# Binary cross entropy with 8-bit targets: VectorE negates both halves of a chunk, and only then clips the next chunk

## The chip, the cores and the metric

The kernel runs on one core of a Trainium2 chip. The metric is the device time of one execution in microseconds (us), shown as the median of several runs. A profile is taken of one more execution.

## The reference

For two float32 arrays of 8192 x 8192, `pred` in (0, 1) and `target` of zeros and ones, the kernel computes the binary cross entropy of every element:

```python
def reference(pred, target):
    eps = 1e-7
    pred = np.clip(pred, eps, 1 - eps)
    return -(target * np.log(pred) + (1 - target) * np.log(1 - pred))
```

As `target` is 0 or 1, one of the two products is always zero. The result is -log(p) where the target is 1 and -log(1 - p) where it is 0. The kernel uses this: |target - 1 + p| is p for a target of 1, and 1 - p for a target of 0, so one logarithm per element is enough.

## The kernel before

**Tiling.** Both inputs and the output are taken as one flat run of 128 x 524288 elements and cut into 35 chunks, k = 0 to 34. The first and the last have 8704 elements per partition (`SIDE`), the 33 between them 15360 (`WIDE`). Each chunk is worked on in two halves (`PARTS = 2`), of 7680 elements per partition in a wide chunk and of 4352 in the two short ones.

**Buffers.** `ring_p` holds three chunks of float32 side by side; chunk k lies in slot k mod 3, is changed in place through all its steps, and is stored from there. `ring_t` is one single chunk of targets in uint8: the transfer that loads the targets turns float32 into 8-bit integers on its way, so it reads 7680 KB and writes 1920 KB for a wide chunk.

**Steps of one chunk.** `clip` (line 85, VectorE) limits p to the allowed interval. `merge` (line 91, VectorE) adds target - 1 to it; then ScalarE takes the absolute value (line 94) and the logarithm (line 95). `negate` (line 99, VectorE) multiplies by -1. `store` (line 70) writes the chunk out.

**Who issues transfers.** Nearly all transfers are issued by GpSimd (POOL), one after another in the order in which the program names them: `load_t` (line 67), `store` (line 70), `load_p` (line 63) and the main part of `store_last` (line 74). They all go into queue q0. Only the first load of `pred` is issued by ScalarE, and the last 1024 columns of the last store by SyncE in three pieces (line 77).

**The order by hand.** The program is written in a manual schedule: each engine executes its instructions in the order of the text, and only waits for what it needs. Before the loop, chunk 0 is clipped. The loop over k = 0 to 34 then does, in this order:

1. both merges of chunk k, with the two ScalarE operations behind each;
2. `load_t(k + 1)` on POOL, which must wait until both merges have read the single target buffer;
3. on VectorE, for each half i: `clip(k + 1, i)`, then `negate(k, i)` (lines 118 to 121);
4. on POOL, `store(k)`, which waits for both negations, and then `load_p(k + 2)`, which waits for the store of chunk k - 1, the last user of its slot.

So the first clip in point 3 waits for the load of `pred` of chunk k + 1, and a negation waits for the logarithm of its half. As VectorE works in order, a negation also waits for every clip that stands in front of it.

**The end.** From chunk 32 on the order differs. The store of chunk 32 is not issued in its own step but in the next, between the loads of the two halves of the last chunk's targets (lines 114 to 117). The stores of chunks 33 and 34 come behind the loop (lines 126 and 127).

Of the kernel before, what the change touches and what calls it, by code (L numbers as in the profile page):

```python
# [1 line left out]

# [4 lines left out]

EPS = 1e-7

WIDE = 15360  # L10
SIDE = 8704
SLOTS = 3
PARTS = 2
REST = 1024
ROWS = (108, 12, 8)


@with_exitstack
def kernel(
    ctx: ExitStack,  # L20
    tc: tile.TileContext,
    pred: bass.AP,
    target: bass.AP,
    out: bass.AP,
):
    nc = tc.nc
    fp32 = mybir.dt.float32
    uint8 = mybir.dt.uint8
    Alu = mybir.AluOpType
    Act = mybir.ActivationFunctionType  # L30
    P = nc.NUM_PARTITIONS

    R, C = pred.shape
    total = R * C // P
    n = (total - 2 * SIDE) // WIDE + 2
    widths = [SIDE] + [WIDE] * (n - 2) + [SIDE]
    assert sum(widths) == total
    last = n - 1

    pool = ctx.enter_context(tc.tile_pool(name="rings", bufs=1))  # L40
    ring_p = pool.tile([P, SLOTS * WIDE], fp32, name="ring_p", tag="ring_p")
    ring_t = pool.tile([P, WIDE], uint8, name="ring_t", tag="ring_t")
    warm = pool.tile([1, 8], fp32, name="warm", tag="warm")

    def chunk(ap, k):
        flat = ap.rearrange("r c -> (r c)")
        start = sum(widths[:k]) * P
        return flat[start : start + widths[k] * P].rearrange("(p w) -> p w", p=P)

    def p_of(k, a=0, b=None):  # L50
        c = k % SLOTS * WIDE
        return ring_p[:, c + a : c + (widths[k] if b is None else b)]

    def t_of(k, a=0, b=None):
        return ring_t[:, a : widths[k] if b is None else b]

    def part(k, i):
        w = widths[k]
        return i * w // PARTS, (i + 1) * w // PARTS

    def load_p(k):
        queue = nc.scalar if k == 0 else nc.gpsimd
        queue.dma_start(out=p_of(k), in_=chunk(pred, k))  # L63

    def load_t(k, *cols):
        cols = cols or (0, widths[k])
        nc.gpsimd.dma_start(out=t_of(k, *cols), in_=chunk(target, k)[:, cols[0] : cols[1]])  # L67

    def store(k):
        nc.gpsimd.dma_start(out=chunk(out, k), in_=p_of(k))  # L70

    def store_last():
        w = SIDE - REST
        nc.gpsimd.dma_start(out=chunk(out, last)[:, :w], in_=p_of(last, 0, w))  # L74
        r = 0
        for rows in ROWS:
            nc.sync.dma_start(
                out=chunk(out, last)[r : r + rows, w:], in_=p_of(last, w)[r : r + rows, :]
            )
            r += rows  # L80
        assert r == P

    def clip(k, i):
        p = p_of(k, *part(k, i))
        nc.vector.tensor_scalar(  # L85
            out=p, in0=p, scalar1=EPS, scalar2=1 - EPS, op0=Alu.max, op1=Alu.min
        )

    def merge(k, i):
        p, t = p_of(k, *part(k, i)), t_of(k, *part(k, i))  # L90
        nc.vector.scalar_tensor_tensor(  # L91
            out=p, in0=t, scalar=1.0, in1=p, op0=Alu.subtract, op1=Alu.add
        )
        nc.scalar.activation(out=p, in_=p, func=Act.Abs)  # L94
        nc.scalar.activation(out=p, in_=p, func=Act.Ln)  # L95

    def negate(k, i):
        p = p_of(k, *part(k, i))
        nc.vector.tensor_scalar(out=p, in0=p, scalar1=-1.0, scalar2=None, op0=Alu.mult)  # L99

    with tc.manual_schedule():
        load_p(0)
        load_t(0)
        load_p(1)
        nc.vector.memset(warm, 1.0)  # L105
        nc.scalar.activation(out=warm, in_=warm, func=Act.Ln)  # L106
        for i in range(PARTS):
            clip(0, i)
        for k in range(n):
            for i in range(PARTS):  # L110
                merge(k, i)
            if k < last - 1:
                load_t(k + 1)
            elif k == last - 1:
                load_t(last, 0, SIDE // PARTS)
                store(last - 2)
                load_t(last, SIDE // PARTS, SIDE)
            for i in range(PARTS):
                if k < last:
                    clip(k + 1, i)  # L120
                negate(k, i)
            if k < last - 2:
                store(k)
            if k < last - 1:
                load_p(k + 2)
        store(last - 1)
        store_last()


# [1 line left out]
_INS = ['pred', 'target']  # L131
_OUTS = [((8192, 8192), 'float32')]


# [23 lines left out]
```

## Time and profile before

| | |
|---|---|
| time, median of 3 runs | 1917.45 us (1916.74 to 1917.89) |
| the profiled execution's own time | 1917.1 us |
| its span, first to last instruction | 1915.1 us |
| VectorE (DVE) busy | 1113.2 us (58%) |
| ScalarE (ACT) busy | 899.8 us (47%) |
| GpSimd (POOL) busy | 57.6 us (3%) |
| bytes read from and written to HBM | 536.87 MB and 268.44 MB |

In the groups of instructions, a row names the line, the engine, the operation, what it writes and reads, and its count; then the total busy time and the mean of one instruction in ns. A row of the timeline gives the start and the duration in us, and in brackets how long the engine stood idle before it and what ended the wait. Where equal instructions follow each other, the timeline merges them into one row and gives their number behind an x. A row of a transfer's issue in the timeline is the time that POOL took to issue it, and not the time of the transfer. The latter stands in the list of transfers, as the median time from issue to landing, with the size in KB on the SBUF side. That list can be taken for a short window as well, and then speaks of the one transfer that was issued in it. In the list of waits, a row names who waited for whom, the total in us, how many times, and the longest.

### The profile page before, as it was taken

To read this page: it belongs to the slowest core of one execution; us is meant where nothing else is said; L and a number is where in the kernel's file an instruction comes from. 1 tells how busy PE (TensorE), PEld (TensorE's weight loads), DVE (VectorE), ACT (ScalarE), POOL (GpSimd) and SP (SyncE) were. 2 spreads that over 40 slices of the span, in tenths; PEclk is the share of its full clock that TensorE was granted. 3 is DMA by queue.
4 is the path that set the end of the run, shared out by engine and by line. 5 is a ranking of instruction groups with operands and counts; after the bars stand their busy time and mean duration, and the time that the engine had idled before them with its cause. 6 is when DMAs were issued, how large, how long until landed. Compare 5 with 4: busy or idle time off the path is not lost.

```text
span 1915.1 us, 651 instructions
## 1 busy us (share of the span) xinstructions
DVE 1113.2 (58%) x211; ACT 899.8 (47%) x142; POOL 57.6 (3%) x109
## 2 busy tenths in 40 slices
DVE  4656655555666555566655556665555666555583
ACT  3554334555433455543345554334555433455543
POOL 0000000000000000000000000000000000000000
DMA  9999999999999999999999999999999999999997
GB/s 296 303 350 299 296 308 300 311 354 349 308 287 308 308 303 354 351 306 303 305 295 308 349 354 304 307 308 287 308 354 349 323 287 308 308 287 354 352 281 290
DMA packets 15428, 604.02 MB, mean 315 GB/s; under 512 B 1728, under 2 KB 1728, under 8 KB 2112
## 3 DMA queue, kind: packets, MB, share of 16 engines
q0 software_dynamic: 15120, 599.01, 98.5%
q10 hardware_dynamic: 144, 4.46, 0.6%
q1 hardware_dynamic: 160, 0.52, 0.1%
q14 instruction: 4, 0.03, 0.0%
HBM read 536.87 MB, written 268.44 MB: 421 GB/s over the span
## 4 chain that ended last, share of the span: by engine, by line
DMA 67%; issue 30%; DVE 1%; POOL 0%; POOLq 0%; DVEq 0%; PEldq 0%
DMA ring_t<-in_target_dram 67%; DVE ring_p L91 1%; POOL ring_t L67 0%; POOL out_dram L70 0%; POOLq L153 0%; POOLq L67 0%; POOLq L70 0%; DVEq L91 0%; PEldq L153 0%; POOLq L74 0%
## 5 line engine op out<-in xcount | busy, mean ns | idle before, releaser
L94 ACT ACTIVATE ring_p<-ring_p 128x7680 f32<-128x7680 f32 (+1 forms) x70 | 450.5, 6436 | 991.1 <-DVE ring_p L91 991.1
L85 DVE TENSOR_SCALAR ring_p<-ring_p 128x7680 f32<-128x7680 f32 (+1 forms) x70 | 283.9, 4057 | 701.9 <-DMA ring_p<-in_pred_dram 701.9
L91 DVE SCALAR_TENSOR_TENSOR ring_p<-ring_t,ring_p 128x7680 f32<-128x7680 uint8 (+1 forms) x70 | 554.1, 7956 | 63.1 <-DMA ring_t<-in_target_dram 63.1
L95 ACT ACTIVATE ring_p<-ring_p 128x7680 f32<-128x7680 f32 (+1 forms) x70 | 451.1, 6444 | 2.2
L99 DVE TENSOR_SCALAR ring_p<-ring_p 128x7680 f32<-128x7680 f32 (+1 forms) x70 | 283.8, 4054 | 17.8 <-ACT ring_p L95 17.8
L70 POOL DMA_DIRECT2D out_dram<-ring_p x34 | 18.3, 538 | 1183.5 <-DVE ring_p L99 1183.5
L67 POOL DMA_DIRECT2D ring_t<-in_target_dram x36 | 20.8, 579 | 631.9 <-DVE ring_p L91 631.1
L63 POOL DMA_DIRECT2D ring_p<-in_pred_dram x34 | 18.0, 530 | 2.6 <-DMA out_dram<-ring_p 2.6
L106 ACT ACT_TABLE_LOAD x1 | 1.3, 1283 | 1.1 <-PEq L142 1.1
L74 POOL DMA_DIRECT2D out_dram<-ring_p x1 | 0.5, 538 | 21.8 <-DVE ring_p L99 21.8
L105 DVE MEMSET warm<- 1x8 f32 x1 | 0.1, 65 | 0.8 <-PEq L142 0.8
L106 ACT ACTIVATE warm<-warm 1x8 f32<-1x8 f32 x1 | 0.2, 208 | 0.0
L142 POOL MEMSET const-float32-0.0<- 128x1 f32 x1 | 0.1, 99 | 0.2 <-issue 0.2
L142 POOL MEMSET const-bfloat16-1.0<- 128x1 bf16 x1 | 0.1, 102 | 0.0
L142 POOL MEMSET const-float32-1.0<- 128x1 f32 x1 | 0.1, 99 | 0.0
L142 POOL MEMSET const-uint8-127<- 128x1 uint8 x1 | 0.1, 99 | 0.0
## 6 DMA issues: line engine op xcount, KB each, us to landing
ring_p<-in_pred_dram POOLq DMA_DIRECT2D x33, 7680.0 KB, 38.5
out_dram<-ring_p POOLq DMA_DIRECT2D x33, 7680.0 KB, 20.9
ring_t<-in_target_dram POOLq DMA_DIRECT2D x33, 1920.0 KB, 39.1
ring_p<-in_pred_dram ACTq DMA_DIRECT2D x1, 4352.0 KB, 20.8
out_dram<-ring_p POOLq DMA_DIRECT2D x1, 4352.0 KB, 16.2
ring_p<-in_pred_dram POOLq DMA_DIRECT2D x1, 4352.0 KB, 46.3
out_dram<-ring_p POOLq DMA_DIRECT2D x1, 3840.0 KB, 12.9
ring_t<-in_target_dram POOLq DMA_DIRECT2D x1, 1088.0 KB, 22.9
```

The source lines that it names most:

```text
L63: queue.dma_start(out=p_of(k), in_=chunk(pred, k))
L67: nc.gpsimd.dma_start(out=t_of(k, *cols), in_=chunk(target, k)[:, cols[0] : cols[1]])
L70: nc.gpsimd.dma_start(out=chunk(out, k), in_=p_of(k))
L74: nc.gpsimd.dma_start(out=chunk(out, last)[:, :w], in_=p_of(last, 0, w))
L85: nc.vector.tensor_scalar(out=p, in0=p, scalar1=EPS, scalar2=1 - EPS, op0=Alu.max, op1=Alu.min)
L91: nc.vector.scalar_tensor_tensor(out=p, in0=t, scalar=1.0, in1=p, op0=Alu.subtract, op1=Alu.add)
L94: nc.scalar.activation(out=p, in_=p, func=Act.Abs)
L95: nc.scalar.activation(out=p, in_=p, func=Act.Ln)
L99: nc.vector.tensor_scalar(out=p, in0=p, scalar1=-1.0, scalar2=None, op0=Alu.mult)
L105: nc.vector.memset(warm, 1.0)
L106: nc.scalar.activation(out=warm, in_=warm, func=Act.Ln)
L142: nc = _bacc.Bacc("TRN2", target_bir_lowering=False, num_devices=1)
```

## The change

On VectorE, the two negations of chunk k now come first, in a loop of their own, and the two clips of chunk k + 1 behind them. Before, clips and negations took turns, with a clip first.

```diff
             for i in range(PARTS):
-                if k < last:
+                negate(k, i)
+            if k < last:
+                for i in range(PARTS):
                     clip(k + 1, i)
-                negate(k, i)
             if k < last - 2:
                 store(k)
             if k < last - 1:
```

The instructions are the same, in number and in shape. The order on POOL, ScalarE and SyncE is the same as before. What each instruction waits for is the same too: a negation for the logarithm of its half, the first clip for the load of its chunk, the store for both negations.

## The prediction

> **What bounds the kernel now.** I read the page first (busy shares, queues, transfers), then the waits, then the timeline of one step in the middle. The page and the waits:
>
> ```profile
> span 1915.1 us, 651 instructions
> DVE 1113.2 (58%) x211; ACT 899.8 (47%) x142; POOL 57.6 (3%) x109
> ...
> q0 software_dynamic: 15120, 599.01, 98.5%
> ...
> ring_p<-in_pred_dram POOLq DMA_DIRECT2D x33, 7680.0 KB, 38.5
> out_dram<-ring_p POOLq DMA_DIRECT2D x33, 7680.0 KB, 20.9
> ring_t<-in_target_dram POOLq DMA_DIRECT2D x33, 1920.0 KB, 39.1
> ...
> ring_p<-in_pred_dram POOLq DMA_DIRECT2D x1, 4352.0 KB, 46.3
> ```
> ```profile
> POOL out_dram L70 <- DVE ring_p L99: 1183.5, 33, 37.6
> POOL ring_p L63 <- DMA out_dram<-ring_p: 2.6, 1, 2.6
> ```
>
> No compute engine is near full. Queue q0, which POOL fills, has packets under way for 98.5% of 16 engines' span: the kernel is a stream of three transfers a step (store k, load of pred k+2, load of target k+1), and time can be won only where one of them takes longer than its bytes need. The long wait of stores on the negations (1183.5 us) is therefore not a price by itself. Loads of pred hardly ever wait for their slot (2.6 us, once). One step, from one landing of the targets to the next:
>
> ```profile
> 944.15 16.23 DVE L91 SCALAR_TENSOR_TENSOR ring_p<-ring_t,ring_p 128x7680 f32<-128x7680 uint8 x2 [1.77 <-DMA ring_t<-in_target_dram]
> ...
> 960.67 0.53 POOL L67 DMA_DIRECT2D ring_t<-in_target_dram  x1 [16.94 <-DVE ring_p L91]
> ...
> 972.10 6.60 ACT L95 ACTIVATE ring_p<-ring_p 128x7680 f32<-128x7680 f32 x1
> 981.71 4.16 DVE L85 TENSOR_SCALAR ring_p<-ring_p 128x7680 f32<-128x7680 f32 x1 [21.34 <-DMA ring_p<-in_pred_dram]
> ...
> 993.92 4.15 DVE L99 TENSOR_SCALAR ring_p<-ring_p 128x7680 f32<-128x7680 f32 x1
> 998.37 0.54 POOL L70 DMA_DIRECT2D out_dram<-ring_p  x1 [37.17 <-DVE ring_p L99]
> 998.90 0.53 POOL L63 DMA_DIRECT2D ring_p<-in_pred_dram  x1
> 999.85 16.23 DVE L91 SCALAR_TENSOR_TENSOR ring_p<-ring_t,ring_p 128x7680 f32<-128x7680 uint8 x2 [1.77 <-DMA ring_t<-in_target_dram]
> ```
>
> A merge or a clip that waits for a transfer starts with its landing, so its start dates the landing to about 0.1 us. The period is 999.85 - 944.15 = 55.70 us. The load of targets takes 999.85 - 981.71 = 18.14 us behind the load of pred. Store and load of pred together take 981.71 - 944.15 = 37.56. The store issued at 998.37 lands 20.9 us later, at 1019.27; the load of pred issued at 998.90 lands at 1037.4, so it takes 18.1 by itself, and the store the other 19.5. Store and loads move the same 7680 KB on the float side, so **the store takes about 1.4 us more than its bytes**. Its place says why: it is issued 1.5 us before the targets land, after which the queue has nothing else. The last negation waits behind both clips, and these behind the landing of pred at 981.7, though the last logarithm was done at 972.10 + 6.60 = 978.70.
>
> **The change, part by part.** No instruction is added or removed; POOL's, ACT's and SP's orders stay. On VectorE the order clip, negate, clip, negate becomes negate, negate, clip, clip.
>
> *Steady steps.* The second negation starts with the last logarithm, 34.55 us after the targets landed, and ends at 38.7 (one takes 4.15). The clips then end at about 47, still 8 us ahead of the next targets at 55: the clips moved back cost nothing. The store can be issued at 39 and no later than 47.5 in place of 54.2, so it is queued well before the targets ahead of it land. The load of pred behind it comes as early; its slot was left by the store before, which landed near 20. The next load of targets is still issued when the merges end, with 36 us of transfers queued.
>
> What a queued store costs is seen at the start, where the first store was issued 5.8 us before the targets landed:
>
> ```profile
> 42.34 4.16 DVE L85 TENSOR_SCALAR ring_p<-ring_p 128x7680 f32<-128x7680 f32 x1 [6.78 <-DMA ring_p<-in_pred_dram]
> ...
> 55.53 0.54 POOL L70 DMA_DIRECT2D out_dram<-ring_p  x1 [19.15 <-DVE ring_p L99]
> ...
> 61.32 16.23 DVE L91 SCALAR_TENSOR_TENSOR ring_p<-ring_t,ring_p 128x7680 f32<-128x7680 uint8 x2 [6.08 <-DMA ring_t<-in_target_dram]
> ...
> 89.27 6.60 ACT L95 ACTIVATE ring_p<-ring_p 128x7680 f32<-128x7680 f32 x1
> 89.74 4.16 DVE L85 TENSOR_SCALAR ring_p<-ring_p 128x7680 f32<-128x7680 f32 x1 [12.19 <-DMA ring_p<-in_pred_dram]
> ...
> 106.40 0.54 POOL L70 DMA_DIRECT2D out_dram<-ring_p  x1 [28.03 <-DVE ring_p L99]
> ...
> 107.81 16.23 DVE L91 SCALAR_TENSOR_TENSOR ring_p<-ring_t,ring_p 128x7680 f32<-128x7680 uint8 x2 [1.71 <-DMA ring_t<-in_target_dram]
> ```
>
> The load of targets ahead of that store took 61.32 - 42.34 = 18.98, so 0.84 more than the 18.14 above; store (4352 KB) and load of pred behind it took 89.74 - 61.32 = 28.42. With 18.1 us for 7680 KB, a full store adds 3328/7680 x 18.1 = 7.84: 36.26. A step with a queued store is then 18.98 + 36.26 = 55.24 us against 55.70: **0.46 us won**. The queue is never empty, but the loss doesn't vanish: 0.84 of the 1.4 moves in front of the store. Ends for this price come from the tail, where one store was queued early and one came just in time:
>
> ```profile
> 1799.65 0.53 POOL L63 DMA_DIRECT2D ring_p<-in_pred_dram  x1 [2.62 <-DMA out_dram<-ring_p]
> ...
> 1835.70 16.23 DVE L91 SCALAR_TENSOR_TENSOR ring_p<-ring_t,ring_p 128x7680 f32<-128x7680 uint8 x2 [1.78 <-DMA ring_t<-in_target_dram]
> ...
> 1844.15 0.53 POOL L67 DMA_DIRECT2D ring_t<-in_target_dram  x1 [43.98 <-DVE ring_p L91]
> 1844.67 0.54 POOL L70 DMA_DIRECT2D out_dram<-ring_p  x1
> 1851.85 2.42 DVE L85 TENSOR_SCALAR ring_p<-ring_p 128x4352 f32<-128x4352 f32 x1
> 1852.22 2.16 POOL L67 DMA_DIRECT2D ring_t<-in_target_dram  x1 [7.01 <-DVE ring_p L91]
> ...
> 1861.24 2.42 DVE L85 TENSOR_SCALAR ring_p<-ring_p 128x4352 f32<-128x4352 f32 x1
> ...
> 1870.29 4.16 DVE L99 TENSOR_SCALAR ring_p<-ring_p 128x7680 f32<-128x7680 f32 x1 [6.63 <-ACT ring_p L95]
> 1874.37 9.29 DVE L91 SCALAR_TENSOR_TENSOR ring_p<-ring_t,ring_p 128x4352 f32<-128x4352 uint8 x2
> 1874.75 0.54 POOL L70 DMA_DIRECT2D out_dram<-ring_p  x1 [20.36 <-DVE ring_p L99]
> ...
> 1897.11 0.54 POOL L74 DMA_DIRECT2D out_dram<-ring_p  x1 [21.82 <-DVE ring_p L99]
> ```
> ```profile
> ring_t<-in_target_dram POOLq DMA_DIRECT2D x1, 544.0 KB, 9.6
> ```
> ```profile
> out_dram<-ring_p POOLq DMA_DIRECT2D x1, 7680.0 KB, 27.3
> ```
> ```profile
> ring_t<-in_target_dram POOLq DMA_DIRECT2D x1, 544.0 KB, 24.9
> ```
> ```profile
> out_dram<-ring_p POOLq DMA_DIRECT2D x1, 7680.0 KB, 20.4
> ```
>
> The load of pred issued at 1799.65 lands at 1845.95 (46.3), the first target part at 1844.15 + 9.6 = 1853.75, the early store at 1844.67 + 27.3 = 1871.97: the target part took 7.8 us for bytes worth 544/1920 x 18.1 = 5.1, a loss of 2.7, some of it from its own late issue; the store then took 18.2. The second target part lands at 1852.22 + 24.9 = 1877.12 (5.15, no loss) and the store issued 2.4 us before that, at 1874.75, lands at 1895.15: 18.03, no loss. So the cost of the meeting of targets and store lies between 0 and 2.7; I take 0.84, since the first step has the same full target load and the same lead of several us. In 30 steps (stores 2 to 31): **-13.8 us**.
>
> *Step 1.* Its last logarithm ends at 89.27 + 6.60 = 95.87, so the negation ends at 100.0 and the clips at 108.2, after the landing near 107.7. The row at 1852.22 shows what happens to an issue under a clip: 2.16 us, not 0.53, and done at 1854.38, just after the clip's end at 1854.27. If both clips hold the store back, it goes out at 108.3, not 106.40: +1.9; if it gets out between them, -0.4. I take +1.
>
> The Trainium skill speaks against this change here: SBUF — State Buffer, Who interferes with whom, says that VectorE in a mode that takes both ports and GpSimd, which writes the descriptors, lock each other out for a whole instruction. The trace agrees (2.16 against 0.53); by the rule alone this part is +1.9, and a steady store goes out near 47.5, still in time.
>
> *The tail.* Now the clips of the last chunk stand in gaps of VectorE, at 1851.85 and 1861.24. After the change both come behind the last negation of the chunk before, bound by its logarithm to 1870.29, and so ahead of the merge at 1874.37: two clips of 2.42, overlapped by under 0.1 each, put it at 1879.1. Everything to the last store hangs on it, and the store before landed at 1895.15, ahead of 1897.11, so nothing covers it: **+4.7 us**.
>
> *Sum.* -13.8 + 1 + 4.7 = -8.1. The profiled run took 1917.1 (the span and 2.0 around it), 0.35 under the median: 1909.0 from the one, 1909.4 from the other. I say 1909.
>
> **The rivals.**
> (a) *The loss only moves.* If the meeting of targets and a full queued store costs 1.3 rather than 0.84, the steps stay at 55.7 and step 1 and the tail remain: 1917.45 + 5.7 = 1923. For it: the 2.7 in the tail. Against it: the first step.
> (b) *The store keeps its 1.4 us and the targets pay as well*: slower. Its place is the end of the store: the next load of targets is issued 16.5 us after the landing, while the store's last packets run; the first step is no test, its 4352 KB store being done by then. From 0.46 more per step at the meeting than the store gives back, it decides. With all of the 1.4 kept, a step is 0.84 longer: 1917.45 + 25.2 + 5.7 = 1948; with half of it gone, about 0.4 longer: 1935. Against it: the stores at the end took 18.0 to 18.2, but no target load was issued during their last 2 us.
> (c) *Nothing is lost at the meeting*, as with the last store: 1.4 x 30 = 42 won, 5.7 paid: 1881.
> That the store isn't issued earlier is excluded by the order, and a lock that lasts through merges too by the issues of 0.53 and 0.54 at 1844.15 and 1844.67, in the middle of the two merges that run from 1835.70 to 1851.93.
>
> **How the numbers follow.** Forecast 0.55, its own range 1905 to 1914 (0.33 to 0.55 per step, step 1 by its ends); (a) 0.22, from 1916 to 1926; (b) 0.17; (c) 0.06. The range 1903 to 1930 leaves out (c) and most of (b). A change under 0.2% (3.8 us, so 1913.6 to 1921.3) can hardly be told from none. Faster: 0.47 of the forecast and (c), 0.53. Same: 0.08 of the forecast and 0.10 of (a), 0.18. Slower: the rest of (a) and (b), 0.29.
>
> **What would show it.** Right: a period near 55.2; stores issued 39 to 47.5 us after the targets land, with issues stretched to several us under clips; the load of targets at 19.0, the store near 18.1; the merge of the last chunk 4.7 us later behind its clips. Wrong: a period of 55.7 with a load of targets above 19.3 (a); a store still at 19.5 beside a load of targets at 19 (b); a target load at 18.1 (c); a store 1 issued before 106 would drop the +1.

## The result, and the profile after

The changed kernel takes **1882.49 us** (median of 5 runs, 1881.71 to 1883.87) against 1916.96 us for the kernel before (median of 5, 1916.74 to 1917.89). The ratio is 0.982, with a 95% interval of 0.9805 to 0.9834. The forecast was 1909 us, with a range of 1903 to 1930: the direction was right, the size far too small. The time is that of rival (c).

The page of the changed kernel, with the lines that answer to those of before:

```profile
span 1880.5 us, 651 instructions
DVE 1116.4 (59%) x211; ACT 899.9 (48%) x142; POOL 278.6 (15%) x109
...
q0 software_dynamic: 15120, 599.01, 98.7%
...
L70 POOL DMA_DIRECT2D out_dram<-ring_p x34 | 127.2, 3742 | 716.5 <-DVE ring_p L99 716.5
...
L63 POOL DMA_DIRECT2D ring_p<-in_pred_dram x34 | 131.8, 3877 | 1.3 <-DMA out_dram<-ring_p 1.3
```

The queue's share is 98.7%, where it was 98.5%. This share says nothing about a gain of 34 us: a packet counts as under way for as long as it lasts, also when it takes 3.1 us in place of 2.27 (such packets are shown at the end of the experiments). POOL's issues of stores and loads of pred have become seven times as long (3742 and 3877 ns in place of 538 and 530), and the kernel is faster all the same. One step in the middle, in the timeline of the changed kernel, and the three transfers that were issued in it, in the list of transfers of that stretch (KB, and us from issue to landing):

```profile
926.91 16.23 DVE L91 SCALAR_TENSOR_TENSOR ring_p<-ring_t,ring_p 128x7680 f32<-128x7680 uint8 x2 [7.47 <-DMA ring_t<-in_target_dram]
...
961.50 4.16 DVE L99 TENSOR_SCALAR ring_p<-ring_p 128x7680 f32<-128x7680 f32 x1 [8.97 <-ACT ring_p L95]
965.58 8.23 DVE L85 TENSOR_SCALAR ring_p<-ring_p 128x7680 f32<-128x7680 f32 x2
965.96 3.89 POOL L70 DMA_DIRECT2D out_dram<-ring_p  x1 [22.00 <-DVE ring_p L99]
969.84 4.08 POOL L63 DMA_DIRECT2D ring_p<-in_pred_dram  x1
981.18 16.23 DVE L91 SCALAR_TENSOR_TENSOR ring_p<-ring_t,ring_p 128x7680 f32<-128x7680 uint8 x2 [7.37 <-DMA ring_t<-in_target_dram]
...
997.70 0.53 POOL L67 DMA_DIRECT2D ring_t<-in_target_dram  x1 [23.77 <-DVE ring_p L91]
```
```profile
out_dram<-ring_p POOLq DMA_DIRECT2D x1, 7680.0 KB, 33.3
ring_p<-in_pred_dram POOLq DMA_DIRECT2D x1, 7680.0 KB, 47.5
ring_t<-in_target_dram POOLq DMA_DIRECT2D x1, 1920.0 KB, 37.7
```

The period is 981.18 - 926.91 = 54.27 us. The targets land at 981.1, the store at 965.96 + 33.3 = 999.3, the load of pred at 969.84 + 47.5 = 1017.3, the next targets at 997.70 + 37.7 = 1035.4: **three transfers of 18.1 us, and nothing lost between them**. It was not so from the start. The merges of the first steps, in the same timeline:

```profile
108.13 16.21 DVE L91 SCALAR_TENSOR_TENSOR ring_p<-ring_t,ring_p 128x7680 f32<-128x7680 uint8 x2
163.56 16.23 DVE L91 SCALAR_TENSOR_TENSOR ring_p<-ring_t,ring_p 128x7680 f32<-128x7680 uint8 x2 [8.55 <-DMA ring_t<-in_target_dram]
218.84 16.23 DVE L91 SCALAR_TENSOR_TENSOR ring_p<-ring_t,ring_p 128x7680 f32<-128x7680 uint8 x2 [8.38 <-DMA ring_t<-in_target_dram]
273.76 16.23 DVE L91 SCALAR_TENSOR_TENSOR ring_p<-ring_t,ring_p 128x7680 f32<-128x7680 uint8 x2 [8.02 <-DMA ring_t<-in_target_dram]
328.04 16.23 DVE L91 SCALAR_TENSOR_TENSOR ring_p<-ring_t,ring_p 128x7680 f32<-128x7680 uint8 x2 [7.38 <-DMA ring_t<-in_target_dram]
```

The first periods are 55.43, 55.28, 54.92 and 54.28 us. So a step is at first shorter than 55.7 by about the 0.46 that was forecast, and then by more; from step 11 on, all periods up to the merge of chunk 33 lie between 54.27 and 54.42. From the packets of the trace one can see what changes meanwhile. In the trace each transfer of queue q0 ends with 16 small packets of 4 bytes, one for each of 16 transfer engines. The time between the first and the last of these 16 packets, at the end of each load of targets, is the *spread* of the engines:

```
chunk of the targets:   1     2     3     4     5     6     7     8     9    10  ...  20    33
spread before, us     0.85  0.85  0.44  0.50  0.42  0.42  0.44  0.52  0.47  0.51     0.48  0.31
spread after, us      0.86  1.14  1.88  2.75  3.13  3.14  3.27  3.87  3.86  3.86     4.13  3.91
```

Before, from chunk 3 to chunk 33, all 16 engines end a load of targets within 0.3 to 0.6 us of each other, but for one load (0.90 at chunk 12). After, the last comes 4 us behind the first, and the losses fade meanwhile. The 16 are not spread evenly, though: in the load that ends at 981.1, eleven end within 0.94 us, and the other five 2.4 to 4.1 us behind the first.

The sum: from the merge of chunk 2 to that of chunk 33 it took 1835.70 - 107.81 = 1727.89 us before, and 1796.42 - 108.13 = 1688.29 after, 39.6 less in 31 steps. The end took 4.7 more, the start 0.3 more: together -34.6, which is the difference of the spans.

### The profile page after: what moved, and what is told of

It is laid out like the page before. It is cut to its first block, busy times and chain, and to the rows that moved or that the text cites. A ratio compares the mean times of both kernels' runs of the same rounds, so it can differ in the third digit from the quotient of the medians.

```text
span 1880.5 us, 651 instructions
## 1 busy us (share of the span) xinstructions
DVE 1116.4 (59%) x211; ACT 899.9 (48%) x142; POOL 278.6 (15%) x109
## 3 DMA queue, kind: packets, MB, share of 16 engines
q0 software_dynamic: 15120, 599.01, 98.7%
## 4 chain that ended last, share of the span: by engine, by line
DMA 65%; issue 30%; DVE 2%; ACT 1%; POOL 1%; POOLq 0%; DVEq 0%; PEldq 0%
DMA ring_t<-in_target_dram 65%; DVE ring_p L91 2%; ACT ring_p L95 1%; ACT ring_p L94 1%; POOL out_dram L70 0%; DVE ring_p L99 0%; POOL ring_p L63 0%; POOL ring_t L67 0%; POOLq L154 0%; POOLq L67 0%; POOLq L70 0%; DVEq L91 0%; PEldq L154 0%; POOLq L74 0%
## 5 line engine op out<-in xcount | busy, mean ns | idle before, releaser
L70 POOL DMA_DIRECT2D out_dram<-ring_p x34 | 127.2, 3742 | 716.5 <-DVE ring_p L99 716.5
L63 POOL DMA_DIRECT2D ring_p<-in_pred_dram x34 | 131.8, 3877 | 1.3 <-DMA out_dram<-ring_p 1.3
L74 POOL DMA_DIRECT2D out_dram<-ring_p x1 | 0.5, 536 | 24.9 <-DVE ring_p L99 24.9
## 6 DMA issues: line engine op xcount, KB each, us to landing
ring_t<-in_target_dram POOLq DMA_DIRECT2D x33, 1920.0 KB, 37.7
```

## The experiments

Theory A, as it was first stated: the engines lose time when all of them turn from one transfer to the next at the same moment. A store that comes as the targets land finds them idle and starts them together, in each step; queued stores let them drift apart. Theory B: the queue ran dry ahead of the store, and that alone was the loss. In the diffs below "-" is the changed kernel, but for the last one, where it is nolock.

**One late store (late_once).** The order of before, in step 17 alone.

```diff
-            for i in range(PARTS):
-                negate(k, i)
+            if k == 17:
+                for i in range(PARTS):
+                    clip(k + 1, i)
+                    negate(k, i)
+            else:
...
```

> The changed kernel, with the order of before (clip, negate, clip, negate) in step 17 alone, so that one store is issued just as the targets ahead of it land. Theory A (out of step): the 16 transfer engines each lose time when all turn from one transfer to the next at the same moment; a late store brings them into step, and they drift apart again over the steps behind it. Then the periods behind step 17 rise from 54.35 to about 55.3 and fall back over 5 to 9 steps as they did at the start, the spread of the engines at the targets' end drops from about 4 us to 0.5 and grows again, and the time is 1886 to 1892 us. Theory B (dry queue): the store lost 1.4 us only because the queue ran empty in front of it; then one period grows by at most 2 us, the next are 54.35 at once, and the time is 1883 to 1885 us.

Measured: 1888.45 us in one run. Its timeline behind the late store:

```profile
981.01 16.23 DVE L91 SCALAR_TENSOR_TENSOR ring_p<-ring_t,ring_p 128x7680 f32<-128x7680 uint8 x2 [1.77 <-DMA ring_t<-in_target_dram]
...
1037.62 16.23 DVE L91 SCALAR_TENSOR_TENSOR ring_p<-ring_t,ring_p 128x7680 f32<-128x7680 uint8 x2 [9.72 <-DMA ring_t<-in_target_dram]
...
1092.85 16.23 DVE L91 SCALAR_TENSOR_TENSOR ring_p<-ring_t,ring_p 128x7680 f32<-128x7680 uint8 x2 [8.32 <-DMA ring_t<-in_target_dram]
...
1147.80 16.23 DVE L91 SCALAR_TENSOR_TENSOR ring_p<-ring_t,ring_p 128x7680 f32<-128x7680 uint8 x2 [8.05 <-DMA ring_t<-in_target_dram]
```

The periods are 56.61, 55.23, 54.95, and on as 54.70, 54.94, 54.97, 54.83, 54.28. The spread falls from 4.17 to 0.56 us with the late store and grows again as 1.05, 1.42, 1.83, 2.43, 2.89, 3.35. All stores behind step 17 were as early as in the steps with 54.35, so the loss in the steps behind a late store isn't the lateness of their own stores. This is what A says, and B does not.

**Every fourth store late (late_fourth).** The same with `if k % 4 == 1 and k < last - 1`.

> The changed kernel, with the order of before in every fourth step (k = 1, 5, ... 29: 8 late stores). Theory A (out of step): each late store brings the engines into step, and the three steps behind it pay about 1.1, 0.9 and 0.6 us as at the start, besides about 1.4 for the late step itself: 8 x 4 = 32 us less what the start pays anyway, 1904 to 1914 us. Theory B (dry queue): 8 x 1.4 = 11 us, 1892 to 1895 us.

Measured: 1909.01 us (1907.43 to 1909.61; ratio to before 0.9957, 0.9940 to 0.9974). Eight late stores, of 33 of full size, take back 26.5 of the 34.5 us. B as the only loss falls.

**The tail by itself (tail_back).** `if k == last - 1` in place of `k == 17`.

> The changed kernel, with the order of before in step 33 alone, the last step with clips. Both theories of the steady steps say the same; the term of the tail (two clips of 2.42 us put in front of the last chunk's merge, +4.7) says 1882.5 - 4.7 = 1877.8 us, and the merge of the last chunk at once behind the last negation of the chunk before. If the tail is covered by transfers, it stays at 1882.5 us.

Measured: 1877.95 us (1876.75 to 1878.41; ratio 0.9793, 0.9778 to 0.9808), 4.5 below the changed kernel. From the merge of chunk 33 to that of chunk 34 its timeline has 38.67 us, as before, and the changed kernel 43.35. This version beats both kernels.

**A spread made by hand (spread, spread8).** Small loads at the start, into a slot that is overwritten later, give some engines more work. spread8 has one of 8 rows:

```diff
         load_p(1)
+        nc.gpsimd.dma_start(
+            out=ring_p[0:32:4, 2 * WIDE : 3 * WIDE], in_=chunk(pred, 2)[:8, :]
+        )
```

> The changed kernel with seven small loads of 4 rows each put behind the second load of pred, into a slot that is overwritten later, so that the 16 transfer engines get 4.5, 3, 1.5 and 0 us of extra work in groups of four, in front of the first full step. Theory A (out of step): the engines start about 3 to 5 us apart, so the periods of steps 2 to 9 are 54.3 to 54.7 from the beginning, and not 55.4, 55.3, 54.9 as in the changed kernel, which pays 3.5 us more there than in its late steps; against it stand about 2.3 to 4.5 us of extra transfers, so the time is 1881 to 1885 us. Theory B (dry queue): the early periods stay as they are in the changed kernel and the time is 1884.5 to 1887 us.

> The changed kernel with one small load of 8 rows behind the second load of pred, into partitions 0, 4, ... 28 of a slot that is overwritten later, so that 8 of the 16 transfer engines get one packet of about 2.3 us more. Theory A (out of step): the engines meet the first store 2.5 to 3.5 us apart and not 0.86; the periods of the steps up to the ninth are together 1.5 to 3.5 us shorter than in the changed kernel, against up to 2.3 us of extra transfer: 1880 to 1883.5 us. Theory B (dry queue): the periods stay as they were and the time is 1883 to 1885 us.

Both expectations missed. spread took 1912.72 us (1910.01 to 1915.67): its seven loads of four neighbouring rows were themselves far slower than thought, as the list of transfers shows for the stretch in which they were issued,

```profile
ring_p<-in_pred_dram POOLq DMA_DIRECT2D x2, 240.0 KB, 55.3
ring_p<-in_pred_dram POOLq DMA_DIRECT2D x2, 160.0 KB, 58.4
```

so that the first steps came 26 us late. spread8 took 1887.06 us (1885.54 to 1889.54), 4.6 more than the changed kernel; its early periods (55.48, 54.66, 54.54, 55.17, 55.68, then 54.5 and less) were no shorter, though the spread began at 2.72. In spread the engines were 3.3 us apart at chunk 3 and 7.5 at chunk 25, and the periods from step 3 on were still 54.3 to 55.0. One way to read spread8 is that two groups of eight, each in step, still turn together; it wasn't tried apart from that. How wide the spread is, is at best a rough measure of the loss, and that a spread takes the loss away was not brought about by hand.

**How early must the store be (dose0, dose3840, dose5760).** VectorE negates one half, clips both halves of the next chunk, in two of the kernels clips 3840 or 5760 of its elements again, and then negates the other half.

```diff
-            for i in range(PARTS):
-                negate(k, i)
+            negate(k, 0)
             if k < last:
                 for i in range(PARTS):
                     clip(k + 1, i)
+                clip_again(k + 1, 3840)
+            negate(k, 1)
```

> VectorE's order is negate first half, clip both halves, negate second half, so that the store is issued about 48.8 us after the targets land, some 5.5 us ahead of the next landing, and the last chunk's clips stand in a gap again. Theory A (out of step): the transfer engines can drift apart until the first of them ends its targets when the store's descriptors come, which allows about 4 us, as wide as they drift anyway: periods of 54.35 after the first ten steps, and 1876 to 1881 us with the tail's 4.7 us won back. Theory B (dry queue): the same.

> As dose0, with a quarter of the next chunk clipped a second time ahead of the last negation (the result is the same), which delays the store by 2.1 us: its descriptors come about 2 us before the last engine ends its targets. Theory A (out of step): the spread of the engines is cut to about 2 us in each step, where the late kernels lost 0.3 to 0.5 us per step: periods of 54.6 to 54.9, 1884 to 1895 us. Theory B (dry queue): the last engine never finds its queue empty, so 1876 to 1881 us, as dose0.

> As dose3840, with 5760 elements clipped again, which delays the store by 3.1 us; its descriptors come about 1 us before the last engine ends. Theory A (out of step): the spread is cut to about 1 us, where 0.5 to 0.9 us per step are lost: periods of 54.9 to 55.3, 1890 to 1908 us. Theory B (dry queue): the last engine never finds its queue empty, 1876 to 1882 us.

Measured: 1890.98 (1888.04 to 1892.54), 1897.41 (1896.47 to 1899.49) and 1903.90 us (1902.69 to 1907.13). The later the store, the slower, though by its packets the last engine never stood idle in front of the store for more than 0.02 us in these steps; B falls again, and A gave the third and nearly the second. dose0 missed both theories by 10 us. Its timeline:

```profile
976.50 4.15 DVE L99 TENSOR_SCALAR ring_p<-ring_p 128x7680 f32<-128x7680 f32 x1
980.94 0.54 POOL L70 DMA_DIRECT2D out_dram<-ring_p  x1 [31.65 <-DVE ring_p L99]
981.47 0.53 POOL L63 DMA_DIRECT2D ring_p<-in_pred_dram  x1
987.18 16.23 DVE L91 SCALAR_TENSOR_TENSOR ring_p<-ring_t,ring_p 128x7680 f32<-128x7680 uint8 x2 [6.53 <-DMA ring_t<-in_target_dram]
```

By its packets the first engine ends these targets 4.0 us before the last, at 982.8. A store whose issue ends at 981.48 comes hardly ahead of that, and from step 20 on the periods alternate between about 54.35 and 55.3 to 55.8. So A was sharpened: the store must be there well before the *first* engine ends, or, so the reading, the leaders are gathered. But dose0 differs from the changed kernel in two more ways: clips run ahead of the last negation (rival C), and the issues take 0.54 us in place of 3.89, since no clip holds POOL (rival D).

**Half and half (late_half).** The order of before from step 17 on (`if 16 < k < last`).

> The changed kernel up to step 16, the order of before from step 17 on. Theory A (in step): the periods fall to 54.35 in the first half, one period at the seam is longer by 1 to 3 us, and from there they are 55.7 at once, since each late store gathers the 16 engines again within about 0.5 us; with the tail as before (4.7 back) the time is 1878 + 15 x 1.35 + 2 = 1900 us, 1897 to 1903. Theory B (dry queue): the same periods, and no gathering, that is a spread that stays near 4 us at the targets' end.

Measured: 1898.34 us (1898.03 to 1900.02). The seam, in its timeline:

```profile
927.03 16.23 DVE L91 SCALAR_TENSOR_TENSOR ring_p<-ring_t,ring_p 128x7680 f32<-128x7680 uint8 x2 [7.47 <-DMA ring_t<-in_target_dram]
981.32 16.23 DVE L91 SCALAR_TENSOR_TENSOR ring_p<-ring_t,ring_p 128x7680 f32<-128x7680 uint8 x2 [1.78 <-DMA ring_t<-in_target_dram]
1037.03 16.23 DVE L91 SCALAR_TENSOR_TENSOR ring_p<-ring_t,ring_p 128x7680 f32<-128x7680 uint8 x2 [1.77 <-DMA ring_t<-in_target_dram]
```

54.29 us, then 55.71 at once and for good, with a spread of 3.97 and then 0.38. The seam itself cost nothing extra, against the 1 to 3 us expected.

**Early and fast (nolock, gap, and again nolock2, gap2).** A filler of about 1.9 us behind the last negation should let POOL issue fast: with both negations first (nolock, with the tail of tail_back), or with the last negation between the two clips (gap).

```diff
+    def pause():
+        nc.vector.scalar_tensor_tensor(
+            out=idle, in0=idle, scalar=1.0, in1=idle, op0=Alu.mult, op1=Alu.max
+        )
...
+                for i in range(PARTS):
+                    negate(k, i)
+                if k < last - 2:
+                    pause()
+                if k < last:
...
```

> As tail_back, with the small operation of about 1.9 us between the two negations and the two clips, so that POOL issues store and load of pred in 0.53 us each, at about 39 us, and not under the clips in 3.9 and 4.1 us. If the lock of VectorE's clips on POOL costs nothing, since a store is needed only some 50 us after the landing: POOL busy falls from about 270 to 60 us and the time stays at 1878 us within 2 us. If the slow issue costs something: faster by 0.1 us or more per step, 1875 us or less.

> The second negation stands between the two clips of the next chunk, and behind it a small operation on one partition (about 1.9 us) that leaves POOL free to issue store and load of pred; they go out about 45 us after the targets land, where dose0 had them at 48.8 and the changed kernel at 39 to 47. Theory A, sharpened by dose0 (a store must be there before the first engine ends its targets, some 50 us after the landing, or the leading engines wait and turn together): the store is 3.5 us ahead of that, so the periods are 54.35 without the alternation of dose0, and with half of the tail's price (one clip of 2.42 ahead of the last merge) the time is 1879 to 1882 us. Rival C (the clips ahead of the last negation cost the time in dose0 by themselves, by when they run, not by the store's issue): periods of 54.9 as in dose0, and 1890 to 1893 us.

Measured: 1893.49 (1892.64 to 1896.66) and 1896.40 us (1895.07 to 1898.71). All expectations missed, as the filler did the contrary. Timeline of nolock:

```profile
972.51 2.00 DVE L91 SCALAR_TENSOR_TENSOR idle<-idle 1x1792 f32<-1x1792 f32 x1
972.89 9.89 POOL L71 DMA_DIRECT2D out_dram<-ring_p  x1 [21.99 <-DVE ring_p L105]
974.45 8.21 DVE L86 TENSOR_SCALAR ring_p<-ring_p 128x7680 f32<-128x7680 f32 x2
982.77 0.53 POOL L64 DMA_DIRECT2D ring_p<-in_pred_dram  x1
```

The filler holds POOL too, and then both clips do; the issue of the store ends at 982.78, and the first engine ends its targets at 983.4. In gap the filler and one clip hold it, to 986.01, and the first engine ends at 986.8. That makes them two more late stores, which say nothing on C and D. With a filler of the merge's form, one input in 8 bits and on 128 partitions:

```diff
-            out=idle, in0=idle, scalar=1.0, in1=idle, op0=Alu.mult, op1=Alu.max
+            out=idle, in0=idle8, scalar=1.0, in1=idle, op0=Alu.subtract, op1=Alu.add
```

> As nolock, where the small operation blocked POOL too and the store's issue took 9.9 us, to 49 us after the landing. Now it has the merge's form (128 partitions, one 8-bit input, scratch data, about 1.9 us), beside which POOL issued in 0.53 us in the kernel before. The store is issued at 39 us in 0.53 us and the load of pred right behind it. Theory A, sharpened (all that counts is that the store is there well before the first engine ends its targets, at about 50 us, so that the engines are never gathered again): periods of 54.35 in the late steps and 1878 us, within 2. Rival D (it is the slow issue under the clips, descriptors in two parts some 4 us apart, that keeps the engines out of step): periods of 54.9 to 55.4 and 1888 to 1905 us.

> As gap, with the same operation in place of the one that blocked POOL: the store goes out in 0.53 us at about 45 us after the landing, between the two clips, some 5 us before the first engine ends its targets. Theory A, sharpened: periods of 54.35, 1879 to 1882 us (half of the tail's price is in it). Rival C (clips that run ahead of the last negation cost the time by themselves): periods of 54.9 and 1890 to 1897 us. Rival D (the slow issue): 1888 to 1905 us.

Measured: **1877.96** us (1877.69 to 1878.13; ratio 0.9794, 0.9779 to 0.9809) and 1880.08 us (1879.56 to 1880.39; ratio 0.9804, 0.9788 to 0.9821). Timeline of nolock2:

```profile
965.84 2.02 DVE L92 SCALAR_TENSOR_TENSOR idle<-idle,idle 128x1792 f32<-128x1792 uint8 x1
966.22 0.54 POOL L72 DMA_DIRECT2D out_dram<-ring_p  x1 [21.99 <-DVE ring_p L106]
966.75 0.53 POOL L65 DMA_DIRECT2D ring_p<-in_pred_dram  x1
967.77 8.22 DVE L87 TENSOR_SCALAR ring_p<-ring_p 128x7680 f32<-128x7680 f32 x2
981.43 16.23 DVE L98 SCALAR_TENSOR_TENSOR ring_p<-ring_t,ring_p 128x7680 f32<-128x7680 uint8 x2 [5.44 <-DMA ring_t<-in_target_dram]
```

Both lie where sharpened A put them. nolock2 issues fast and nothing is lost, nor won against tail_back's 1877.95: the slow issue under clips (D) is neither the cause nor a price. gap2 has a clip ahead of the last negation (one, where dose0 has two), and no loss, which speaks against C; its store goes out at 971.76, some 5 us before the first engine ends at 976.7.

**Where the loss stands.** The packets of the traces show it. A packet of a full load of pred or a full store takes 2.27 us, one of the targets 2.28. What differs is the last packet of a transfer, at the turn to the next one. Its mean over the 16 engines, in us:

```
                                   last packet of the targets          last packet of the store
                                   (the store follows)                 (the load of pred follows)
before, steps 2 to 31              2.28                                3.03 to 3.16
late_half, steps 17 to 31          2.28                                3.07 to 3.15
changed kernel, first steps        3.05, 2.30, 2.76, 2.53, 2.50        2.27
changed kernel, steps 22 to 31     2.28                                2.27
late_once, the late store          2.28                                3.15
late_once, the loads behind it     3.20, 2.72, 2.61, 2.32, 2.28, 2.54  2.27
dose3840, dose5760, steps 10 to 31 2.28 to 2.37                        2.63 to 3.09
nolock2, gap2, steps 21 to 31      2.28                                2.27
```

So there are two losses. A late store pays in its own step: in the kernel before, an engine stands idle for 0.36 us in front of it in the mean (this part is theory B's), its first packet takes 0.10 us longer, and its last 0.8 to 0.9. A store in good time pays nothing at its own end, but the targets ahead of it lose up to 0.9 us at theirs, for some steps behind the start or behind a late store. The 56.61 us in late_once hold both, 54.35 + 1.35 + 0.92; at the seam of late_half the next store is late too, and only the first loss is there.

How early the store is queued decides between them. From the end of its issue to the end of the first engine's targets it is 7.3 us in the changed kernel and 4.6 in gap2, in the mean of 30 steps, and the late steps lose nothing; it is 1.3, 0.8 and 0.5 us in dose0, dose3840 and dose5760, which lose 0.5, 0.8 and 1.0 us per step, and 0.0 in the kernel before, which loses 1.4. These are means of steps that differ (0.2 to 3.6 us in dose0), so they give no threshold. The spread alone doesn't decide it: with the engines about 0.5 us apart, step 18 of late_once (0.56, store in time) lost nothing at the store's end, and the store of dose5760 that was issued at 988.72 (0.48) lost 0.6 there. That the drift of the engines is the reason why the other loss fades is therefore an argument, from a spread that grows meanwhile, and not shown.

## Why the prediction was wrong

*What bounds the kernel: right.* It is the stream of three transfers, and the 1.4 us that the store took over its bytes were all that could be won in a step. They were won, in late steps: 55.70 became 54.35.

*Steady steps: the mechanism half right, the price wrong.* Stores do go out 39 us after the landing (965.96 - 926.91), in time and at no cost by the moved clips. The step that failed is "I take 0.84, since the first step has the same full target load and the same lead of several us". That 0.84 was measured right after the start, with the engines close together (spread 0.85), and taken for the price of any queued store. It is the last packet of those targets (3.08 us in place of 2.28), and it goes to nothing within about ten steps, while the engines drift apart. The gain per step was so 1.35 us in late steps and 39.6 / 31 = 1.28 in the mean, and not 0.46: the term of -13.8 us came to -39.6. A row that pointed that way stood in the prediction, as the end at 0 of the cost's range: the last store came in time and lost nothing. It was left at a chance of 0.06, as one case against one; it was no proof either, since it stood behind a load of 544 KB and not a full one.

*Step 1: +1 forecast, 0.3 found.* POOL did get in between the two clips: its store was issued from 100.36 on, for 3.89 us, to just after the first clip, and the load of pred took the second clip's time.

*The tail: right.* The rows of the changed kernel that answer to those of before:

```profile
1831.01 4.16 DVE L99 TENSOR_SCALAR ring_p<-ring_p 128x7680 f32<-128x7680 f32 x1 [8.97 <-ACT ring_p L95]
1835.08 4.76 DVE L85 TENSOR_SCALAR ring_p<-ring_p 128x4352 f32<-128x4352 f32 x2
1835.46 2.16 POOL L70 DMA_DIRECT2D out_dram<-ring_p  x1 [21.99 <-DVE ring_p L99]
1839.77 9.27 DVE L91 SCALAR_TENSOR_TENSOR ring_p<-ring_t,ring_p 128x4352 f32<-128x4352 uint8 x2
```

Two clips stand ahead of the last merge, 43.35 - 38.67 = 4.68 us as forecast (4.7), and tail_back wins them.

*The rivals.* (a) and (b) fell: the load of targets takes 18.1 in late steps and so does the store, although the next load of targets is still issued (997.70) while the store's last packets run. (b) had the place right, since most of what the store lost stood in its last packet, but not the reason: in the changed kernel the next targets are issued there as well, and that packet takes 2.27 us. (c) was right in its time (1881 against 1882.5), in part by luck: it has nothing lost at the meeting in any step, and the first ten steps do lose there.

What stays open is why the last packet at such a turn takes longer, whether in the memory, in the engines or on the way between, and why this fades at the targets' end. The runs show when the loss comes and goes and in which packets it stands, and not what spends it.

## What to carry to other kernels

Where one queue of transfers sets the time, as here, a transfer should be issued well before the *first* of the 16 engines has finished the one ahead of it, some microseconds before the landing that a semaphore reports (in these runs 4.6 us ahead of the first engine was enough, and 1.3, in the mean, was not). A transfer that arrived just in time cost more than its small gap: in the kernel before it started all engines within 0.15 us, and one such store was paid for over several steps (6 us in late_once). A price read from the first steps of a loop is one of a state that may not last, so look for the same row later in the trace, or change a single step in the middle and watch how the periods come back.

## What the runs showed of the hardware

An operation of VectorE with two float32 inputs, on one partition, held POOL's issue until it and the two clips behind it had ended (0.54 us became 9.89), while one of the same length on 128 partitions with one 8-bit input did not (0.54). The two also differ in their arithmetic; which of the differences matters wasn't tried. Behind a negation that ran straight into two clips, POOL got in between the clips (3.89 and 4.08 us); behind the filler it had to wait for both.

Loads of four neighbouring rows were much slower than their bytes: in the packets of the run spread, a row of 61440 bytes took 7.0 to 8.6 us, where it takes 2.27 in a load of 128 rows.
